# Second layer of a streaming encoder: where the output projection of two token tiles stands

## The chip, the cores and the metric

The kernel runs on one core of one Trainium2 chip. The metric is the device time of one launch in microseconds (us). A core has five engines with a queue each: TensorE (PE, matmuls; PEld is its weight load), VectorE (DVE), ScalarE (ACT), GpSimd (POOL) and SyncE (SP, which only issues DMAs). Each executes its instructions in the order in which they stand, and waits for the others by semaphores. In TensorE's accumulators (PSUM, here banks of 128x512 floats) the products arrive; SBUF holds operands; DRAM the inputs, outputs and spilled tiles.

## What is computed

Two layers over 1024 prompt frames and 8 streams of 16 new frames: attention (the first layer with a sliding window, the second over its own and eight earlier chunks of 64 frames), the output projection with a residual, and a squared-ReLU MLP. For the second layer, cut to what matters here:

```python
qp = project_q_b(hp, g_attn[layer], w_q_b[j], g_q_b[j])
ap = band_attention_prompt(qp, kb_p, vb_p, LEFT_CHUNKS_B, rel_fn, None)
hp = hp + ap @ w_o_b[j]
hp = hp + mlp(hp, g_mlp[layer], w_up[layer], w_down[layer])
```

`mlp` begins with an RMS norm over the 1024 features: the mean of squares of a row, its inverse root, and a multiplication with the gain. Results are float32; each operand is split into a rounded high part and the rest, and a product is three matmuls (high x high, high x low, low x high).

## The kernel before

The frames are nine tiles of 128 rows: tiles 0 to 7 of the prompt, tile 8 (`ST`) of the samples. Attention works in 32 groups, one per tile and pair of steps over the four K/V heads: the first 16 groups take heads 0 and 1 of all tiles, the last 16 heads 2 and 3. For a group, scores are computed in two halves (`score_b`, L388: matmuls L400, minimum and bias on DVE L424 to L428, exponentials on ACT L437 and L440, the sum's reciprocal L447, the division on POOL L450), the probabilities are turned by PE (L293), split (ACT L109, DVE L115) and multiplied with V (L300, L301); ACT copies the result (L315) and SP stores it (L320).

The output projection follows the same halves. The half `A` (heads 0 and 1, the first 512 rows of the weight) and the half `B` (the last 512 rows) of a tile each load the stored attention output in two parts (L306, L308), add them (L310), split the sum into `oh` and `ol`, and run 24 matmuls, 12 for each 512 columns (`wo_proj`, L144 to L149). In attention `WO` (L1474) does this: it loads the residual tile (L1497), adds each half row of the product to it on DVE (L1508) and stores it (L1510, on POOL's queue for the half B); its addition L310 and its cast of `oh` (L111) run on POOL. The table `plan` of `CFG` tells after which group a tile's half is taken; what is listed under 32 comes after the last group (`run(work_of(32))`, L1699). Whatever stands in `plan` under B goes into `wo_done`; tiles whose home in `xt` is `keep` stay in SBUF (tiles 0 and 4).

Behind attention comes the passage ahead of the MLP, `wo_phase` (L612). It goes through the nine tiles in the order of `WO_ORDER`, for this layer 0, 4, 1, 5, 6, 2, 7, 3, 8. `O` loads the residual tile (L629) and, if its half B is not done, the attention output. `M` does the missing half B: 24 matmuls into `ps_wo`, two additions on DVE (L653), a store on ACT's queue (L655), and then for every tile the norm (L602): squares on ACT (L605), a small DVE step (L607), the inverse root on POOL (L609) and, in place, the scaling on DVE (L610). When both tiles of a pair (i, i + 4) are ready, `S` forms four sums and differences on POOL (L669 to L672) and `T` turns seven half tiles by PE (L662) and splits them (ACT L109, DVE L115) into `sx`. The up products (L715 to L717) read `sx` and the split weights of the first block, loaded by L743 into `ru` and split into `wq` and `w`.

Nobody writes the order of the instructions by hand: a scheduler puts each engine's work in order from priorities and its own model of durations. The lines that matter for the order are these:

```python
run(work_of(32))
self.wo_done = {t for g in plan for c, t in plan[g] if c == "B"}
```

```python
for n in range(2) if t not in self.wo_done else ():
    nn = slice(n * 512, n * 512 + 512)
    ps = self.psum("m", [P, 512], "ps_wo")
    self.wo_proj(ps, *osp[t], wo, nn)
    nc.vector.tensor_tensor(x[:, nn], ps, x[:, nn], ALU.add)
if t not in self.wo_done:
    nc.scalar.dma_start(self.xd[t], x)
```

Of the kernel before, what the change touches and what calls it, by code (L numbers as in the profile page):

```python
# [1709 lines left out]
def make_plan(tail):  # L1710
    plan = {}
    for s in range(2 * NT):
        if s + 2 < NT:
            plan[2 * s] = [("Q", s + 2)]
        elif s + 2 < 2 * NT:
            plan[2 * s] = [("R", s + 2 - NT)]
        if s + 3 < NT:
            plan[2 * s + 1] = [("K", s + 3)]
    plan[13] = [("R", ST)]
    plan.update(tail)  # L1720
    return plan
# [27 lines left out]
CFG = [  # L1749
    dict(banks=dict(g=(5, 1), s=(2, 1), m=(1, 1)), q_bufs=4, order={}, plan=make_plan({15: [('A', 0)], 17: [('A', 1)], 19: [('A', 2)], 21: [('A', 3)], 23: [('A', 4)], 25: [('A', 5)], 30: [('A', 6)], 31: [('A', 7)], 32: [('A', 8), ('B', 0), ('B', 4), ('B', 3)]}),  # L1750
        la=3, prio=0, xt={('A', 8): 'x', ('B', 3): 'x', ('B', 0): 'keep', ('B', 4): 'keep'}, late=0, eng='cgu', k2=3, q2=9, lead=3, sf=0, up=(99, 2, 0, 3), ld=((10, 10, 11, 11), (11, 12, 13, 14), (27, 28, 29, 30)), n='g', q='g', qrb=1, np=3, bias_bufs=3, p_bufs=3, psp=(), wr='mmmm', wt=(0, 0, 2, 0, 2, 2, 0, 1, 2), rx=1, kd=1, o2=0, sb=0),
    dict(banks=dict(g=(4, 1), s=(3, 1), m=(1, 1)), q_bufs=4, order={}, plan=make_plan({15: [('A', 0)], 17: [('A', 1)], 19: [('A', 2)], 21: [('A', 3)], 23: [('A', 4)], 25: [('A', 5)], 27: [('A', 8)], 28: [('A', 7)], 29: [('A', 6)], 31: [('B', 0), ('B', 4), ('B', 1)], 32: [('B', 5), ('B', 2), ('B', 3)]}),
        la=2, prio=1000, xt={('B', 0): 'keep', ('B', 4): 'keep', ('B', 1): 'hh', ('B', 5): 'hl', ('B', 2): 'hh', ('B', 3): 'hl'}, late=0, eng='Ogu', k2=3, q2=6, lead=9, sf=0, up=(4, 2, 0, 99), ld=((11, 11, 11, 11), (11, 11, 11, 11), (26, 27, 28, 29)), n='g', q='g', qrb=2, np=2, bias_bufs=2, p_bufs=10, psp=(), wr='mmmm', wt=(0, 0, 0, 1, 1, 1, 1, 1, 2), rx=0, kd=1, o2=1, sb=3),
]

TC_KW = dict(schedule_with_timeline_sim=True)
# [42 lines left out]
```

## Time and profile before

| | us |
|---|---|
| three runs, median | 2405.27 |
| lowest and highest | 2404.04, 2407.24 |
| span of the profiled execution, first to last instruction | 2399.3 |

The profile gives the profiled execution by its span alone; its own launch time is not listed, so the 6.0 us between the span and the median stand for what lies around the span. The profile is of one execution. It lists for each engine when an instruction ran, how long it took, and how long the engine stood idle before it, with the instruction or the transfer that ended that idle time. PE's busy share is 97%, DVE's 68%, ACT's 51%, POOL's 22%. The mean granted TensorE clock is 0.992 of full speed.

### The profile page before, as it was taken

To read this page: it belongs to the slowest core of one execution; us is meant where nothing else is said; L and a number is where in the kernel's file an instruction comes from. 1 tells how busy PE (TensorE), PEld (TensorE's weight loads), DVE (VectorE), ACT (ScalarE), POOL (GpSimd) and SP (SyncE) were. 2 spreads that over 40 slices of the span, in tenths; PEclk is the share of its full clock that TensorE was granted. 3 is DMA by queue.
4 is the path that set the end of the run, shared out by engine and by line. 5 is a ranking of instruction groups with operands and counts; after the bars stand their busy time and mean duration, and the time that the engine had idled before them with its cause. 6 is when DMAs were issued, how large, how long until landed. Compare 5 with 4: busy or idle time off the path is not lost.

```text
span 2399.3 us, 33421 instructions
## 1 busy us (share of the span) xinstructions
PE 2320.4 (97%) x11621; PEld 1935.5 (81%) x11621; DVE 1626.3 (68%) x3002; ACT 1217.9 (51%) x2423; POOL 535.6 (22%) x828
## 2 busy tenths in 40 slices
PE   7998999899999999999999999998999999999999
PEld 6786877788888888888777788887888888888887
DVE  6687786755655777776567877877655555776674
ACT  4676675555555433232267666665655555333321
POOL 3343332312112100000333434344211211000000
PEclk9998999999999999999999999999999999999999
DMA  7345546244433874342743555555434435744332
GB/s 244 122 127 168 171 156 200 95 155 158 145 128 141 323 245 146 117 141 99 237 149 111 188 161 173 173 169 174 138 127 145 154 137 200 278 140 158 112 116 114
DMA packets 218457, 385.88 MB, mean 161 GB/s; under 512 B 50408, under 2 KB 125104, under 8 KB 211120
## 3 DMA queue, kind: packets, MB, share of 16 engines
q1 hardware_dynamic: 195136, 307.16, 39.0%
q0 software_dynamic: 21776, 71.84, 7.7%
q10 hardware_dynamic: 1376, 4.74, 0.5%
q8 instruction: 92, 1.51, 0.3%
q14 instruction: 77, 0.63, 0.1%
HBM read 246.47 MB, written 136.14 MB: 159 GB/s over the span
## 4 chain that ended last, share of the span: by engine, by line
PE 82%; DMA 7%; DVE 5%; ACT 2%; issue 2%; POOL 1%; SPq 1%; ACTq 0%; DVEq 0%; POOLq 0%
PE ps_x L715 9%; PE ps_x L717 9%; PE ps_x L716 9%; PE ps_y L717 7%; PE ps_y L716 7%; PE ps_y L715 7%; PE ps_mm L186 3%; PE ps_mm L188 3%; PE ps_mm L187 3%; PE ps_tr L293 2%; PE ps_mm L147 2%; PE ps_mm L149 2%; PE ps_mm L148 2%; PE ps_s L717 1%; PE ps_s L716 1%
## 5 line engine op out<-in xcount | busy, mean ns | idle before, releaser
L109 ACT CAST w<-r 128x2048 fp32r<-128x2048 f32 x56 | 107.1, 1913 | 322.9 <-PE ps_y L717 212.1
L715 PE MATMUL ps_x<-w,s 128*128 128x512 f32 x512 | 199.5, 390 | 2.7 <-DVE hc L854 2.1
L717 PE MATMUL ps_x<-w,s 128*128 128x512 f32 x512 | 199.4, 389 | 0.0
L716 PE MATMUL ps_x<-w,s 128*128 128x512 f32 x512 | 199.2, 389 | 0.0
L186 PE MATMUL ps_mm<-w,hh 128*128 128x512 f32 x432 | 175.0, 407 | 13.8 <-ACT kw L253 5.1
L188 PE MATMUL ps_mm<-w,hl 128*128 128x512 f32 x432 | 174.3, 403 | 1.7 <-DMA hl<-hTd 1.4
L187 PE MATMUL ps_mm<-w,hh 128*128 128x512 f32 x432 | 172.5, 400 | 0.7 <-DVE w L159 0.7
L109 ACT CAST s<-s 128x2048 fp32r<-128x2048 f32 x56 | 107.1, 1913 | 117.9 <-DMA s<-hd 108.6
L115 DVE TENSOR_TENSOR w<-r,w 128x2048 fp32r<-128x2048 f32 x56 | 128.2, 2290 | 51.9 <-ACT w L109 51.9
L715 PE MATMUL ps_x<-sx,w 128*128 128x512 f32 (+1 forms) x408 | 157.8, 387 | 4.6 <-ACT hc L834 2.7
L1021 DVE TENSOR_TENSOR x<-ps_y,x 128x512 f32<-128x512 f32 x136 | 92.3, 687 | 101.1 <-PE ps_y L717 101.0
L717 PE MATMUL ps_x<-sx,w 128*128 128x512 f32 (+1 forms) x408 | 154.1, 378 | 0.0
L716 PE MATMUL ps_x<-sx,w 128*128 128x512 f32 (+1 forms) x408 | 154.1, 378 | 0.0
L109 ACT CAST w<-ru 128x512 fp32r<-128x512 f32 (+1 forms) x160 | 110.0, 708 | 85.3 <-PE ps_y L716 32.0
L717 PE MATMUL ps_y<-w,s 128*128 128x512 f32 x384 | 149.5, 389 | 0.0
L716 PE MATMUL ps_y<-w,s 128*128 128x512 f32 x384 | 149.4, 389 | 0.0
L715 PE MATMUL ps_y<-w,s 128*128 128x512 f32 x384 | 149.4, 389 | 0.0
L115 DVE TENSOR_TENSOR s<-s 128x2048 fp32r<-128x2048 f32 x56 | 128.1, 2287 | 26.5 <-ACT s L109 26.5
L115 DVE TENSOR_TENSOR ptl<-ps_tr,pth 128x512 fp32r<-128x512 f32 x180 | 122.6, 685 | 24.8 <-ACT pth L109 19.0
L115 DVE TENSOR_TENSOR w<-ru,w 128x512 fp32r<-128x512 f32 (+1 forms) x160 | 126.6, 793 | 10.9 <-ACT w L109 10.8
L109 ACT CAST pth<-ps_tr 128x512 fp32r<-128x512 f32 x180 | 104.8, 594 | 47.9 <-PE ps_tr L293 39.3
L115 DVE TENSOR_TENSOR wq<-ru,wq 128x1024 fp32r<-128x1024 f32 x32 | 39.7, 1240 | 131.9 <-ACT wq L109 131.9
(280 smaller groups left out, 6573.3 us busy)
## 6 DMA issues: line engine op xcount, KB each, us to landing
s<-hd SPq DMA_DIRECT2D x56, 1024.0 KB, 4.7
ru<-in_w_up SPq DMA_DIRECT2D x64, 512.0 KB, 3.9
r<-in_w_down SPq DMA_DIRECT2D x32, 1024.0 KB, 5.7
hd<-hc POOLq DMA_DIRECT2D x128, 256.0 KB, 2.7
hd<-hs POOLq DMA_DIRECT2D x96, 256.0 KB, 2.5
x<-xd SPq DMA_DIRECT2D x41, 512.0 KB, 4.6
o<-oTd SPq DMA_DIRECT2D x52, 256.0 KB, 4.1
hTd<-hh SPq DMA_DIRECT2D x36, 256.0 KB, 4.5
```

The lines of the kernel that those rows point to most:

```text
L109: a = nc.scalar.copy(hi, src)
L115: return a, e.tensor_tensor(lo, src, hi.bitcast(F32), ALU.subtract)
L147: nc.tensor.matmul(ps, oh[:, k, :], w[:, 0, k, nn], start=(k == 0), stop=False)
L148: nc.tensor.matmul(ps, oh[:, k, :], w[:, 1, k, nn], start=False, stop=False)
L149: nc.tensor.matmul(ps, ol[:, k, :], w[:, 0, k, nn], start=False, stop=(k == 3))
L186: nc.tensor.matmul(ps, a, w[:, 0, k, :], start=(k == 0), stop=False)
L187: nc.tensor.matmul(ps, a, w[:, 1, k, :], start=False, stop=False)
L188: nc.tensor.matmul(ps, b, w[:, 0, k, :], start=False, stop=(k == KC - 1))
L715: a = mm(ps, ah, bh, start=first, stop=False, skip_group_check=True)
L716: mm(ps, ah, bl, start=False, stop=False, skip_group_check=True)
L717: return a, mm(ps, al, bh, start=False, stop=last, skip_group_check=True)
L1021: tt(xs[t][:, N[n]], ps, xs[t][:, N[n]], ALU.add)
```

## The change

In the second layer's entry of `CFG`, the tiles 2 and 3 of the half B are taken out of `plan` under 32, and their homes out of `xt`. Nothing else is edited. So `WO` is not called for them at the end of attention, they are no longer in `wo_done`, and `wo_phase` does their half B, in its order (6, 2, 7, 3, 8), with its own instructions: the addition of the two parts and the cast of `oh` then run on DVE and ACT, and the store is issued by ACT.

```diff
-    dict(banks=dict(g=(4, 1), s=(3, 1), m=(1, 1)), q_bufs=4, order={}, plan=make_plan({15: [('A', 0)], 17: [('A', 1)], 19: [('A', 2)], 21: [('A', 3)], 23: [('A', 4)], 25: [('A', 5)], 27: [('A', 8)], 28: [('A', 7)], 29: [('A', 6)], 31: [('B', 0), ('B', 4), ('B', 1)], 32: [('B', 5), ('B', 2), ('B', 3)]}),
-        la=2, prio=1000, xt={('B', 0): 'keep', ('B', 4): 'keep', ('B', 1): 'hh', ('B', 5): 'hl', ('B', 2): 'hh', ('B', 3): 'hl'},
...
+    dict(banks=dict(g=(4, 1), s=(3, 1), m=(1, 1)), q_bufs=4, order={}, plan=make_plan({15: [('A', 0)], 17: [('A', 1)], 19: [('A', 2)], 21: [('A', 3)], 23: [('A', 4)], 25: [('A', 5)], 27: [('A', 8)], 28: [('A', 7)], 29: [('A', 6)], 31: [('B', 0), ('B', 4), ('B', 1)], 32: [('B', 5)]}),
+        la=2, prio=1000, xt={('B', 0): 'keep', ('B', 4): 'keep', ('B', 1): 'hh', ('B', 5): 'hl'},
...
```

What the scheduler makes of it shows in the engines' orders. The first place is PE at the end of attention, ahead of the second half of the last group's scores (`ps_sf`, `ps_sn`); `ps_mm` is the projection. Before:

```order
L301 MATMUL ps_pv<-ptl,VS 128x512
L293 MATMUL ps_tr<-identr,p 128x128 x5
L147 MATMUL ps_mm<-w,oh 128x512
L148 MATMUL ps_mm<-w,oh 128x512
L149 MATMUL ps_mm<-w,ol 128x512
...
L400 MATMUL ps_sf<-KT,qT 128x384 x4
L400 MATMUL ps_sn<-KT,qT 128x256 x4
```

And now, at the same place:

```order
L293 MATMUL ps_tr<-identr,p 128x128 x5
L301 MATMUL ps_pv<-ptl,VS 128x512
L400 MATMUL ps_sf<-KT,qT 128x384 x4
L300 MATMUL ps_pv<-pth,VS 128x512
L400 MATMUL ps_sn<-KT,qT 128x256 x4
```

The twelve projection matmuls (three rows shown, repeated four times) no longer stand between the transposes and the scores; the same holds for three more groups of twelve behind them.

The second place is DVE in the passage, where a tile's second addition and its norm stand. Before, `x_17389` is tile 7, `x_17322` tile 2 and `x_17303` tile 6:

```order
L653 TENSOR_TENSOR x_17389<-ps_wo_17512,x_17389 128x512
L653 TENSOR_TENSOR x_17389<-ps_wo_17526,x_17389 128x512
L610 SCALAR_TENSOR_TENSOR x_17322<-x_17322,mrs_17444,gb_11010 128x1024
L610 SCALAR_TENSOR_TENSOR x_17303<-x_17303,mrs_17434,gb_11010 128x1024
L115 TENSOR_TENSOR sx_17188<-ps_n_17296,sx_17187 128x4x128
L115 TENSOR_TENSOR sx_17223<-ps_n_17340,sx_17222 128x4x128
L115 TENSOR_TENSOR sx_17218<-ps_n_17347,sx_17217 128x4x128
L607 TENSOR_SCALAR mms_17544<-mssq_17542 128x1
L610 SCALAR_TENSOR_TENSOR x_17389<-x_17389,mrs_17546,gb_11010 128x1024
```

And now, `x_17223` being tile 6, `x_17242` tile 2 and `x_17318` tile 7:

```order
L310 TENSOR_TENSOR o_17368<-o_17368,o2_17370 128x512
L653 TENSOR_TENSOR x_17242<-ps_wo_17377,x_17242 128x512
L607 TENSOR_SCALAR mms_17361<-mssq_17359 128x1
L610 SCALAR_TENSOR_TENSOR x_17223<-x_17223,mrs_17363,gb_11010 128x1024
L115 TENSOR_TENSOR sx_17108<-ps_n_17216,sx_17107 128x4x128
L115 TENSOR_TENSOR sx_17143<-ps_n_17269,sx_17142 128x4x128
L115 TENSOR_TENSOR sx_17138<-ps_n_17276,sx_17137 128x4x128
L653 TENSOR_TENSOR x_17242<-ps_wo_17391,x_17242 128x512
L115 TENSOR_TENSOR ol_17374<-o_17368,oh_17373 128x512
L653 TENSOR_TENSOR x_17318<-ps_wo_17479,x_17318 128x512
L607 TENSOR_SCALAR mms_17409<-mssq_17407 128x1
L610 SCALAR_TENSOR_TENSOR x_17242<-x_17242,mrs_17411,gb_11010 128x1024
```

Between a tile's second addition and its norm fewer instructions stand than before: two and the small step L607 for tile 2, and the same for tile 7 further on; one addition and L607 for tile 3.

The third place is SP's queue where attention ends (`oTd_1_7_109` is the attention output of tile 7, `xd_113` the residual of tile 2). Before:

```order
L320 DMA oTd_1_7_109<-pvt 64x2x128 x8
L306 DMA o<-oTd_1_7_109 128x512
L588 DMA oTd_1_8_110<-so 128x2x32
L308 DMA o_17393<-oTd_1_7_109 128x512
L743 DMA ru<-in_w_up 128x4x256 x2
L629 DMA x<-xd_113 128x1024
```

And now:

```order
L320 DMA oTd_1_7_109<-pvt 64x2x128 x4
L306 DMA o<-oTd_1_3_105 128x512
L320 DMA oTd_1_7_109<-pvt 64x2x128 x4
L743 DMA ru<-in_w_up 128x4x256 x2
L306 DMA o<-oTd_1_7_109 128x512
L308 DMA o_17322<-oTd_1_7_109 128x512
```

The loads of the up weights moved ahead of those of tile 7's attention output, and a load for tile 3 came in.

## Rows read from the trace of the kernel before

**Rows 1.** The page's first part: busy us, share of the span, instructions.

```profile
PE 2320.4 (97%) x11621; PEld 1935.5 (81%) x11621; DVE 1626.3 (68%) x3002; ACT 1217.9 (51%) x2423; POOL 535.6 (22%) x828
```

**Rows 2.** Busy time by stretch (us from the span's start), tail and passage.

```profile
core 0: us, PE busy (x) PEld busy (x) DVE busy (x) ACT busy (x) POOL busy (x), PEclk, DMA share, GB/s
1600.00:1642.00 42.00, 38.57 (x210) 31.93 (x210) 30.20 (x71) 25.71 (x70) 16.20 (x22) 1.00 0.51 167
1642.00:1664.90 22.90, 22.71 (x122) 18.50 (x121) 16.88 (x25) 11.46 (x22) 13.07 (x10) 1.00 0.70 223
1664.90:1690.80 25.90, 17.46 (x104) 14.07 (x104) 23.03 (x35) 17.05 (x31) 12.50 (x11) 0.87 0.22 78
```

**Rows 3.** PE's timeline in the tail: start, us, instruction, idle before and its end.

```profile
1617.12 0.50 PE L147 MATMUL ps_mm<-w,oh 128*128 128x512 f32 x1 [1.53 <-DVE mms L607]
...
1619.97 0.87 PE L400 MATMUL ps_sf<-KT,qT 128*128 128x384 f32 x4
```

**Rows 4.** Timelines of DVE, ACT and POOL in the tail.

```profile
1627.62 0.69 DVE L310 TENSOR_TENSOR o<-o,o 128x512 f32<-128x512 f32 x1 [2.19 <-DMA o<-oTd]
1629.01 0.17 DVE L447 RECIPROCAL li<-l 128x2 f32<-128x2 f32 x1
1641.08 2.46 DVE L610 SCALAR_TENSOR_TENSOR xo<-xo,mrs,gb 128x1024 f32<-128x1024 f32 x2
1626.48 0.47 ACT L440 ACTIVATE p<-ps_sn,mnb 128x256 f32<-128x256 f32 x1
1637.52 0.59 ACT L109 CAST pth<-ps_tr 128x512 fp32r<-128x512 f32 x1 [2.38 <-PE ps_tr L293]
1629.32 0.61 POOL L1510 DMA_DIRECT2D xd<-xo  x1 [6.50 <-DVE li L447]
1629.98 1.58 POOL L450 TENSOR_SCALAR p<-p,li 128x640 f32<-128x640 f32 x2
```

**Rows 5.** DVE's timeline in the passage: splits of turned tiles.

```profile
1645.54 1.89 DVE L115 TENSOR_TENSOR sx<-ps_n,sx 128x512 fp32r<-128x512 f32 x3 [1.99 <-ACT sx L109]
1691.69 0.69 DVE L115 TENSOR_TENSOR sx<-ps_n,sx 128x512 fp32r<-128x512 f32 x1
```

**Rows 6.** Busy time by stretch: the first layer's whole passage, then the second layer's.

```profile
396.20:457.80 61.60, 55.63 (x313) 46.11 (x311) 49.77 (x74) 31.82 (x56) 26.89 (x24) 1.00 0.43 144
1641.10:1692.30 51.20, 42.20 (x238) 34.28 (x238) 42.31 (x63) 30.37 (x56) 25.57 (x21) 0.93 0.46 151
```

**Rows 7.** SP's and ACT's timelines: tile 7's stores, the up weights' loads and cast.

```profile
1634.67 10.27 SPq L320 DMA_DIRECT2D oTd<-pvt  x8
1647.03 0.92 SPq L743 DMA_DIRECT2D ru<-in_w_up  x2
1651.81 1.06 ACT L109 CAST wq<-ru 128x1024 fp32r<-128x1024 f32 x1
```

**Rows 8.** DVE's additions and norms: tiles 7 and 8, then the first layer.

```profile
1659.80 1.29 DVE L653 TENSOR_TENSOR x<-ps_wo,x 128x512 f32<-128x512 f32 x2 [1.10 <-DMA x<-xd]
1666.38 1.28 DVE L610 SCALAR_TENSOR_TENSOR x<-x,mrs,gb 128x1024 f32<-128x1024 f32 x1 [1.04 <-DMA xd<-x]
1671.79 1.27 DVE L653 TENSOR_TENSOR x<-ps_wo,x 128x512 f32<-128x512 f32 x2
1676.15 1.28 DVE L610 SCALAR_TENSOR_TENSOR x<-x,mrs,gb 128x1024 f32<-128x1024 f32 x1 [0.95 <-DMA xd<-x]
435.20 0.68 DVE L653 TENSOR_TENSOR x<-ps_wo,x 128x512 f32<-128x512 f32 x1
439.59 1.28 DVE L610 SCALAR_TENSOR_TENSOR x<-x,mrs,gb 128x1024 f32<-128x1024 f32 x1 [0.95 <-POOL mrs L609]
```

**Rows 9.** Line 655 in the passage, three stores: us from issue to landing.

```profile
DMA to landing us min/median/max: 2.6/5.2/6.5
```

**Rows 10.** Busy time by stretch, columns as in rows 2: granted clock.

```profile
1660.00:1670.00 10.00, 6.71 (x36) 5.04 (x34) 8.89 (x12) 5.31 (x10) 3.27 (x5) 1.00 0.51 158
1670.00:1680.00 10.00, 8.16 (x43) 7.59 (x44) 8.71 (x14) 4.75 (x9) 6.65 (x6) 0.66 0.13 52
```

More of the change, by code (lines that the diff above doesn't have):

```diff
@@ L1751 @@
         la=3, prio=0, xt={('A', 8): 'x', ('B', 3): 'x', ('B', 0): 'keep', ('B', 4): 'keep'}, late=0, eng='cgu', k2=3, q2=9, lead=3, sf=0, up=(99, 2, 0, 3), ld=((10, 10, 11, 11), (11, 12, 13, 14), (27, 28, 29, 30)), n='g', q='g', qrb=1, np=3, bias_bufs=3, p_bufs=3, psp=(), wr='mmmm', wt=(0, 0, 2, 0, 2, 2, 0, 1, 2), rx=1, kd=1, o2=0, sb=0),
-    dict(banks=dict(g=(4, 1), s=(3, 1), m=(1, 1)), q_bufs=4, order={}, plan=make_plan({15: [('A', 0)], 17: [('A', 1)], 19: [('A', 2)], 21: [('A', 3)], 23: [('A', 4)], 25: [('A', 5)], 27: [('A', 8)], 28: [('A', 7)], 29: [('A', 6)], 31: [('B', 0), ('B', 4), ('B', 1)], 32: [('B', 5), ('B', 2), ('B', 3)]}),
-        la=2, prio=1000, xt={('B', 0): 'keep', ('B', 4): 'keep', ('B', 1): 'hh', ('B', 5): 'hl', ('B', 2): 'hh', ('B', 3): 'hl'}, late=0, eng='Ogu', k2=3, q2=6, lead=9, sf=0, up=(4, 2, 0, 99), ld=((11, 11, 11, 11), (11, 11, 11, 11), (26, 27, 28, 29)), n='g', q='g', qrb=2, np=2, bias_bufs=2, p_bufs=10, psp=(), wr='mmmm', wt=(0, 0, 0, 1, 1, 1, 1, 1, 2), rx=0, kd=1, o2=1, sb=3),
+    dict(banks=dict(g=(4, 1), s=(3, 1), m=(1, 1)), q_bufs=4, order={}, plan=make_plan({15: [('A', 0)], 17: [('A', 1)], 19: [('A', 2)], 21: [('A', 3)], 23: [('A', 4)], 25: [('A', 5)], 27: [('A', 8)], 28: [('A', 7)], 29: [('A', 6)], 31: [('B', 0), ('B', 4), ('B', 1)], 32: [('B', 5)]}),
+        la=2, prio=1000, xt={('B', 0): 'keep', ('B', 4): 'keep', ('B', 1): 'hh', ('B', 5): 'hl'}, late=0, eng='Ogu', k2=3, q2=6, lead=9, sf=0, up=(4, 2, 0, 99), ld=((11, 11, 11, 11), (11, 11, 11, 11), (26, 27, 28, 29)), n='g', q='g', qrb=2, np=2, bias_bufs=2, p_bufs=10, psp=(), wr='mmmm', wt=(0, 0, 0, 1, 1, 1, 1, 1, 2), rx=0, kd=1, o2=1, sb=3),
 ]
```

## Prediction, written before the changed kernel ran

> **What bounds the kernel now.** I read the busy shares first [rows 1]: PE is busy 97% of the span of 2399.3 us, so PE's idle time in the stretch that the change touches is all that can be won or lost, some ten microseconds. Then I cut the second layer's turn from attention to the MLP into three stretches [rows 2]. In the tail of attention (1600 to 1642 us) PE is busy 38.57 of 42.00 us. In the first part of the passage (1642 to 1664.9), where the output projection of tiles 6, 7 and 8 runs, it is busy 22.71 of 22.90. In the second part (1664.9 to 1690.8) it is busy only 17.46 of 25.90, and DVE 23.03: there DVE sets the pace, with the splits of the turned tiles, the norms and the split of the first weights. So the change takes matmuls from a stretch with 3.4 us of idle PE and puts them, with their DVE work, ahead of a stretch that DVE bounds.
>
> **Removed from the tail.** Tiles 2 and 3 have two half rows of 12 matmuls each, 48 in all. Twelve take 2.85 us, from 1617.12 to 1619.97 [rows 3]: 11.4 us of PE together. They did not all lie on the path; three places give something back.
> (a) The first group stands ahead of the last scores. The order shows those scores now right behind the transposes: 2.8 us.
> (b) The last exponentials end at 1626.95, but the division of the probabilities ends only at 1631.56 [rows 4]: DVE sits idle for 2.19 us until 1627.62 for a tile of the projection, adds it, and POOL puts a store of 0.61 us ahead. In the new order none of this is in front of the reciprocal; it needs 0.17 us, the division 1.58 us, and about 0.5 us of hand-overs: 4.6 becomes 2.3, a gain of 2.3 us.
> (c) The last group stands among the transposes of the last head group; ACT waits 2.38 us for them [rows 4]. That goes: 2.4 us.
> Sum 7.5 us. Bounds: at most the whole 11.4; at least 3.8, if (c) is taken up by the two casts that ACT now has there and a norm of 1.28 us that DVE now runs between two score reductions comes off (a) (2.3 + 1.5).
>
> **Removed DMAs.** Two loads of x and two stores on POOL's queue go from the tail; the stores come back on ACT's queue in the passage, and the loads are the ones the passage had anyway. I cost this at nothing beyond (b). The first o load of tile 2 now stands early in SP's queue, held until the first half's last projection matmul; that matmul ends ahead of the store that stands behind it, so nothing waits longer.
>
> **Added to the passage.** I measure it from the two norms of the kept tiles (DVE, 1641.08) to the last split of turned tiles, which ends at 1692.3 [rows 4, 5]: 51.2 us, in which DVE is busy 42.31 and idle 8.9 [rows 6].
> Work: four additions of the projection, one addition of two o halves and one split of it (those of tile 2 fall ahead of 1641.08 in the new order). Three DVE instructions in a row take 1.89 us [rows 5], so 0.63 each: 3.8 us. PE's 11.4 us fit: it is busy 42.2 of 51.2 us now [rows 6].
> Waits at the start: DVE idles 1.99 us for the first turned tile, as before [rows 5]. Its next instruction was an addition; now it is the split of the first up weights. Their load goes out right behind the last stores of tile 7, which end 3.9 us after the start; the cast began 4.8 us after the issue (1647.03 to 1651.81) and takes 1.06 [rows 7], so the split starts near 10.0 us after the start, while DVE is free at 6.3: 3.7 us idle, 5.7 together.
> Waits in front of norms: the norm works in place, so it waits for the store of the same tile and for its own statistics. From the end of the second addition to the norm's start it took 5.3 us for tile 7 (1661.09 to 1666.38) and 3.1 us for tile 8 (1673.06 to 1676.15), both ended by the store, and 3.7 us once in the first layer [rows 8]. The spread is the landing of the stores, 2.6 to 6.5 us [rows 9], longer while loads fly. Before, six instructions or more stood between and little idling was left. Now, by the order, between the second addition and the norm DVE has 2.0 us of work for tile 6, 1.4 for tiles 2 and 7, 0.8 for tile 3 and 3.2 for tile 8. I take 5.3 for tiles 6 and 2, whose stores go out while other tiles load, and 3.1 for 7, 3 and 8, which come when the loads are through: 3.3 + 3.9 + 1.7 + 2.3 + 0 = 11.2 us idle.
> Idle sum 16.9 us against 8.9, so 8.0 more; with the work 11.8 us. Bounds: with 5.3 for all five, 17.7 idle in front of norms and 18.3 us in all. Low: the first layer's passage is the nearest row without such an order; it holds 84 more of these matmuls (20.0 us) and is 61.6 us long instead of 51.2 [rows 6], 0.52 us for each us of PE, which for 11.4 us gives 5.9.
> The row shows landings of 2.6 to 6.5 us. The Trainium skill (DMA: Bandwidth & Descriptors, Anatomy of one DMA) fits a fixed 2.0 us and bytes over 436 GB/s for the software path, an estimate of 3.2 us for 512 KB whatever else flies. By that rule, with 0.4 us to the issue, all five norms would wait 3.6 us, 9.2 us idle, and the time would be 2.0 us less, 2407.6; the longest landing speaks against it.
>
> **Sum.** -7.5 + 11.8 = +4.3 us on the profiled span of 2399.3. The median of the three runs, 2405.27, stands 6.0 us above that span, for what lies around it, and the change does not touch that: 2409.6 us. Only above 0.2% (4.8 us) could a measurement of this kernel tell it from no change, so this lies just inside.
>
> **The rivals.**
> Faster, PE-bound throughout: the whole 11.4 us leaves the tail, and the passage grows as in the first layer, 5.9: -5.5, 2399.8 us. For it: PE is full in the tail and in the first part. Against: the waits of DVE and ACT in the tail [rows 4] are not PE's, and the order puts norms right behind additions.
> Same, with the scheduler's idle filled: tail 7.5, passage 5.9: -1.6, 2403.7 us. For it: DVE has 8.9 us of idle, and the first layer does twice as many tiles with only 11.8.
> Slower, by the stores: loads fly through the whole passage, so every norm waits 5.3 us: -7.5 + 18.3 = +10.8, 2416.1 us. It decides where the store of tiles 7, 3 and 8 lands later than 3.9 us after its issue, halfway. For it: the landing's median of 5.2 us. Against: tile 8's was short.
> Slower, by the clock: between 1660 and 1670 PE was busy 6.71 us of 10, and in the next 10 us the granted clock was 0.66, a mean over the two levels 2.4 and 1.2 GHz [rows 10]. There only turns and 256-wide products stood, off the path. If it falls in the new passage while the projection runs, a third of 10 us is lost to PE, 3.4 us, on top of the forecast: +7.7, 2413.0 us. The Trainium skill (TensorE: Matmul & The Clock Gate, Part 1) says that an idle TensorE is halved and only sustained work gives the clock back; the trace agrees, 0.66 behind idle time.
> That the change does not do what it says is ruled out by the order: 24 matmuls of each of the two tiles now stand behind the end of attention.
>
> **How the numbers follow.** Forecast 0.48, with its own range of 2405 to 2414 (each wait between its short and its long value); faster 0.13; same 0.18; stores 0.11; clock 0.10. The forecast straddles the bound of 4.8 us, a little over half inside: 0.26 same, 0.22 slower. Slower 0.22 + 0.11 + 0.10 = 0.43; same 0.26 + 0.18 = 0.44; faster 0.13. The range of 2402 to 2416 leaves out most of the faster rival and half of the stores', under 0.2.
>
> **What would show it.** The start of the passage (the two kept norms) should come near 1633.6 in the new profile. From there to the last split of turned tiles should be near 63 us, with DVE idle near 17 and rows in which the norm waits for a store of x of tiles 6, 2, 7 and 3. The second half of the last scores should start near 1617. It is wrong if the passage is under 58 us, if its idle time stands in front of other instructions than these norms and the weight split, or if the tail ends where it did.

## The result, and the profile after

| | before | changed |
|---|---|---|
| 22 runs each, median, us | 2403.8 | 2410.8 |
| lowest and highest, us | 2394.6, 2410.6 | 2404.8, 2417.2 |
| ratio, with its 95% interval | | 1.0026 (1.0016 to 1.0036) |
| span of the profiled execution, us | 2399.3 | 2405.7 |

By the ratio the changed kernel is 6.3 us slower (3.9 to 8.7; the medians are 7.0 apart). The forecast was +4.3. The interval is clear of zero, but it does not settle whether the change costs more than 4.8 us, which the prediction took as the least that can be told from no change. The profiled execution of the changed kernel took 2407.47 us by its launch time and 2405.7 by its span, so 1.8 us lie around a span. Of the 6.0 us that the prediction put "around the span", 4.2 are only the distance of that execution from the median.

The page's first part for the changed kernel, then its windows over the end of attention and the passage (columns as in [rows 2]):

```profile
PE 2321.5 (97%) x11621; PEld 1935.2 (80%) x11621; DVE 1630.3 (68%) x3004; ACT 1218.6 (51%) x2425; POOL 531.5 (22%) x822
```

```profile
1623.60:1633.60 10.00, 6.05 (x27) 3.58 (x26) 7.46 (x14) 6.05 (x13) 0.57 (x1) 1.00 0.54 171
1633.60:1638.60 5.00, 4.16 (x20) 3.47 (x21) 3.86 (x5) 2.91 (x8) 2.44 (x2) 0.66 0.40 108
1633.60:1698.30 64.70, 53.98 (x285) 44.14 (x285) 48.84 (x69) 29.47 (x57) 24.88 (x21) 0.92 0.40 137
```

The last line answers to the second of [rows 6]: the passage, from the kept norms to the last split of turned tiles, is 64.7 us long instead of 51.2, with 48.8 us of DVE work instead of 42.3 and 15.9 us of DVE idle time instead of 8.9. The first two lines are new: PE is busy only 6.05 of the last 10 us of attention, and in the next 5 us, the first of the passage, the granted clock is 0.66. Before, both the tail and the first part of the passage stood at 1.00 [rows 2].

What DVE waited for in the passage, in total, times and longest (the view of waits):

```profile
DVE x L610 <- DMA xd<-x: 6.8, 4, 3.7
DVE sx L115 <- ACT sx L109: 4.4, 6, 2.0
DVE wq L115 <- ACT wq L109: 2.4, 1, 2.4
DVE mms L607 <- ACT junk L605: 2.1, 4, 1.0
```

DVE's timeline there, the kept norms and then the norms of tiles 6, 2, 7, 3 and 8, which answer to [rows 8]:

```profile
1633.62 2.46 DVE L610 SCALAR_TENSOR_TENSOR xo<-xo,mrs,gb 128x1024 f32<-128x1024 f32 x2
...
1654.36 1.80 DVE L610 SCALAR_TENSOR_TENSOR x<-x,mrs,gb 128x1024 f32<-128x1024 f32 x1 [1.17 <-DMA xd<-x]
...
1663.97 1.28 DVE L610 SCALAR_TENSOR_TENSOR x<-x,mrs,gb 128x1024 f32<-128x1024 f32 x1 [3.67 <-DMA xd<-x]
...
1670.39 1.98 DVE L610 SCALAR_TENSOR_TENSOR x<-x,mrs,gb 128x1024 f32<-128x1024 f32 x1 [0.99 <-DMA xd<-x]
...
1677.49 1.95 DVE L610 SCALAR_TENSOR_TENSOR x<-x,mrs,gb 128x1024 f32<-128x1024 f32 x1 [0.99 <-DMA xd<-x]
...
1688.06 1.28 DVE L610 SCALAR_TENSOR_TENSOR x<-x,mrs,gb 128x1024 f32<-128x1024 f32 x1
```

The chain of work that ended last, from tile 6's second addition on (start, us, what):

```profile
1650.74 0.61 DVE x L653
...
1651.37 2.90 DMA xd<-x
...
1656.09 1.87 DVE sx L115 x3
1657.96 0.61 DVE x L653
...
1658.60 5.29 DMA xd<-x
...
1665.18 1.88 DVE sx L115 x3
1667.06 0.61 DVE x L653
...
1667.69 2.61 DMA xd<-x
...
1672.29 1.88 DVE sx L115 x3
1674.16 0.61 DVE x L653
...
1674.80 2.60 DMA xd<-x
...
1677.49 1.95 DVE x L610
```

It is one figure four times over: second addition, store, its landing, norm in place, three splits, next second addition. The landings alone are 13.4 us of the chain. The longest is tile 2's store (5.29), the only one under which loads of x flew (tiles 3 and 8, issued at 1655.11 and 1657.62).

### The profile page after: what moved, and what is told of

It is laid out like the page before. It is cut to its first block, busy times and chain, and to the rows that moved or that the text cites. A ratio compares the mean times of both kernels' runs of the same rounds, so it can differ in the third digit from the quotient of the medians.

```text
span 2405.7 us, 33408 instructions
## 1 busy us (share of the span) xinstructions
PE 2321.5 (97%) x11621; PEld 1935.2 (80%) x11621; DVE 1630.3 (68%) x3004; ACT 1218.6 (51%) x2425; POOL 531.5 (22%) x822
## 4 chain that ended last, share of the span: by engine, by line
PE 80%; DMA 8%; DVE 6%; ACT 3%; issue 2%; POOL 1%; SPq 1%; ACTq 0%; DVEq 0%; POOLq 0%
PE ps_x L715 9%; PE ps_x L717 9%; PE ps_x L716 9%; PE ps_y L716 7%; PE ps_y L717 7%; PE ps_y L715 7%; PE ps_mm L186 3%; PE ps_mm L188 3%; PE ps_mm L187 3%; PE ps_tr L293 2%; PE ps_mm L147 2%; PE ps_mm L149 1%; PE ps_mm L148 1%; PE ps_s L717 1%; PE ps_s L716 1%
## 5 line engine op out<-in xcount | busy, mean ns | idle before, releaser
L115 DVE TENSOR_TENSOR w<-r,w 128x2048 fp32r<-128x2048 f32 x56 | 128.3, 2291 | 52.2 <-ACT w L109 52.2
L115 DVE TENSOR_TENSOR w<-ru,w 128x512 fp32r<-128x512 f32 (+1 forms) x160 | 126.6, 794 | 11.3 <-ACT w L109 11.2
```

Of the source, the lines that this page charges most:

```text
L115: return a, e.tensor_tensor(lo, src, hi.bitcast(F32), ALU.subtract)
```

## The experiments

Executions differ by 15 us in the time at which the same instructions ahead of the change run, so the spans of two profiles say little. The table counts from one reciprocal of attention's sums (L447, the eighth from the last; 1572.15 us in the first profile of before, 1568.85 in that of the change) to the kept norms, then the passage, and then to L845, the MLP's first addition into `ps_y`. "Timed" is the ratio times the median of before in the same comparison, with its interval.

| kernel | kept norms at | passage | L845 at | timed against before, us |
|---|---|---|---|---|
| before, two profiles | 68.9, 68.1 | 51.3, 49.8 | 124.1, 121.8 | |
| the change, two profiles | 64.8, 64.6 | 64.7, 63.2 | 133.8, 132.0 | +6.3 (3.9 to 8.7) |
| tail alone | 65.5 | 55.8 | 127.0 | -1.4 (-4.6 to +1.9) |
| no store | 64.8 | 59.6 | 130.1 | +1.7 (-1.7 to +5.1) |
| before, no store | 68.9 | 51.9 | 124.7 | +1.0 (-2.2 to +4.3) |
| norm later | 64.5 | 56.9 | 127.0 | +2.9 (-0.2 to +6.0) |
| additions late | 63.8 | 63.9 | 132.1 | +9.8 (6.5 to 13.0) |
| tile 3 alone | 68.0 | 56.0 | 129.8 | +4.1 (1.4 to 7.0) |
| tile 6 too | 69.3 | 52.7 | 125.8 | +3.8 (0.5 to 7.4) |
| before, norm later | 69.5 | 52.4 | 125.8 | +3.1 (0.0 to 6.2) |
| tile 6 and norm later | 68.0 | 53.4 | 125.3 | +4.6 (1.9 to 7.2) |

From L845 to the end of the span it is 703.0 to 703.6 us in every profile: nothing behind is changed. Three of the kernels leave something out: tail alone the half B of tiles 2 and 3, the two without stores the stored residual of the second layer's passage.

**The two kernels once more.**

> The changed kernel itself, profiled once more, to see how far one execution speaks for the others. Counted from the third but last group's reciprocal of the sum (L447, the 57th of the execution), the kept norms came at 64.8 us, the last split of turned tiles ended at 129.4 and the MLP's first addition into ps_y (L845) stood at 133.8. Stores theory: kept norms within 1 us of that, the end within 3 us, as the landing of four stores varies; the half clock at the start of the passage comes again. Rival, the 3.7 us wait for tile 2's store was an accident: the end comes 3 us or more earlier.

> The kernel before, profiled once more: from the same reciprocal the kept norms came at 68.9 us, the last split ended at 120.2 and L845 stood at 124.1. Expected within 1.5 us of these. If L845 comes at 127 or later, the first profile was a lucky one and the change costs 6 us there, not 9.7.

The kept norms came within 0.8 us and the passages within 1.5 us of their first profiles; only L845 of the kernel before was off by more than named, 2.3 us earlier, which makes the difference no smaller. The clock over its passage was 0.97 instead of 0.93. In the changed kernel the clock fell again at the start of the passage, to 0.52 in its first 5 us. The wait for tile 2's store is no accident; the second profile has it at 4.53 us:

```profile
1671.14 1.28 DVE L610 SCALAR_TENSOR_TENSOR x<-x,mrs,gb 128x1024 f32<-128x1024 f32 x1 [4.53 <-DMA xd<-x]
```

By these profiles the change takes 3.8 us from the tail, adds 13.4 to the passage and 0.4 behind it: +9.9, more than the timed +6.3. That two profiles of each kernel stand above the interval of the timed runs stays open. So it is for two variants: at L845, tail alone stands 4.0 us and no store 7.1 us behind the mean of before, against -1.4 and +1.7 timed. The profiles are used below for where the time goes, the timed runs for what a version costs.

**The tail alone.**

```diff
+            if layer:
+                self.wo_done |= {2, 3}
```

> The changed kernel, with the half B of tiles 2 and 3 left out altogether (their residual lacks heads 2 and 3); they pass through the passage like tiles 1 and 5. It weighs the tail of attention alone. Stores theory (the tail gives 7.5 us, the passage takes 13.5 because each norm of a moved tile stands behind the store of its own tile): the two kept norms start near 1633.6, the passage is 49 to 52 us long, as before the change (51.2) or less by the wait of tile 2, and the time is 7.5 to 9 us under the kernel before. Rival, the start of the passage (the first split of up weights now waits 2.4 us for its load, which would stay here): the passage stays 54 us or longer and the time is 3 to 5 us under.

Neither number was met. The kept norms came 3.1 us earlier than before (65.5 against the mean of 68.5), not 7.5, and the passage was 55.8 us long though it had nothing of tiles 2 and 3 to compute. Its windows, two in the tail and then three from the passage on:

```profile
1622.97:1627.97 5.00, 3.56 (x17) 2.85 (x17) 4.17 (x14) 3.81 (x11) 0.61 (x1) 0.82 0.31 118
1627.97:1632.97 5.00, 4.96 (x26) 3.68 (x24) 2.71 (x7) 3.61 (x13) 2.21 (x4) 0.84 0.62 170
...
1643.00:1648.00 5.00, 4.20 (x18) 3.54 (x19) 3.82 (x5) 2.69 (x7) 2.48 (x3) 0.53 0.35 85
1643.00:1698.80 55.80, 43.77 (x229) 36.50 (x230) 45.76 (x63) 30.12 (x56) 26.82 (x21) 0.84 0.41 139
1693.00:1703.00 10.00, 7.40 (x40) 6.53 (x39) 7.28 (x12) 5.15 (x11) 0.00 (x0) 0.66 0.65 211
```

The granted clock fell in the tail itself, to 0.82 and 0.84; it is 0.53 in the first 5 us of the passage, 0.84 over the passage instead of 0.93 [rows 6], and 0.66 where the MLP's products begin. But what grew in the passage is above all DVE's work: 63 instructions, as many as before, keep it busy 45.8 us instead of 42.3 [rows 6], and it idles 10.0 us instead of 8.9. Three norms of 1.28 us took 2.10, 2.27 and 2.04 us beside sums that POOL forms; the next runs show this more plainly. So this run does not weigh the tail by itself, and what the clock alone cost in it is not shown. The rival had the right length, but for another reason: the split of the first weights did not wait in this run. 11.4 us of PE work left out of the program gave 1.4 us, with zero inside the interval.

**Without the stores**, in the changed kernel and in the kernel before.

```diff
-                if t not in self.wo_done:
+                if t not in self.wo_done and not layer:
                     nc.scalar.dma_start(self.xd[t], x)
```

> The changed kernel without the store of the residual in the second layer's passage (tiles 6, 2, 7, 3, 8), so that nothing holds the norm back but its own statistics; the second layer's last addition then reads a residual without half B of these tiles. Stores theory: the four waits of norms (6.8 us of DVE's idle time) shrink to the 0.9 us or so of the statistics' way over ACT and POOL, PE gets its turns earlier, and the time falls by 4 to 7 us against the changed kernel, so near the kernel before (0 to +2 us). Rival, the added work (DVE's six instructions and PE's 11.4 us set the length whatever the stores do): it falls by less than 1.5 us, +5 us against the kernel before.

> The kernel before, without the same stores (tiles 6, 7, 8). Stores theory: it has two waits of 1.0 us behind stores, of which the statistics would leave a part, so it gains 0 to 2 us against itself. Rival, the stores cost by their traffic (they slow the loads of x that fly beside them): it gains 3 us or more, since tile 2's load, on the chain for 9.7 us, lands earlier.

The changed kernel lost 4.6 us of its 6.3, as the stores theory said, though the two intervals overlap and L845 came only 2.8 us earlier. The kernel before gained nothing that can be seen, so no cost of the stores' traffic by itself shows. But the passage was still 59.6 us long, with DVE's idle time down to 8.6 us and its busy time up to 51.0:

```profile
1643.70:1703.30 59.60, 52.33 (x280) 42.81 (x281) 51.00 (x69) 29.55 (x57) 24.74 (x21) 0.93 0.32 105
```

The norms, no longer held back, now ran into the sums that POOL forms. One of four such pairs, DVE's row and then POOL's:

```profile
1663.65 2.31 DVE L610 SCALAR_TENSOR_TENSOR x<-x,mrs,gb 128x1024 f32<-128x1024 f32 x1
```

```profile
1663.58 1.29 POOL L672 TENSOR_TENSOR s<-x,s 128x512 f32<-128x512 f32 x1
```

The norm takes 1.28 us where POOL is idle, and here 2.31: the rest of POOL's sum (until 1664.87) and 1.09 us behind it.

**The norm later.** `M` and the norm are separated, so that a tile's norm is written behind the next tile's projection, and ordered on DVE behind its second addition:

```diff
-                M(t)
+                M(m)
+                N(t, m)
...
+            def N(t, m):
+                    y = self.norm(small, work.tile([P, D], mybir.dt.bfloat16, tag="junk", name="junk"), xs[t])
+                        self.behind(added[m], y)
```

> The changed kernel; in the second layer the norm of a stored tile is ordered behind the second addition of the next tile (an order of DVE's instructions only, no buffer and no instruction added), so that 2 to 5 us of other work stand between a store and its norm. Stores theory: the waits of 1.2, 3.7, 1.0 and 1.0 us go, the passage is 58 to 61 us instead of 64.7, and the time is 4 to 7 us under the changed kernel, within 2 us of the kernel before. Rival, the added work: same length, 64 us, +6 us. Second rival, turns that come later: the norm and with it the turns of a pair come 2 us later each, PE runs out of projection at the end, and the time is over the changed kernel's.

One wait of 1.21 us for a store is left of four, and the passage is 56.9 us, shorter than expected. The second rival fell: no buffer and no work was taken away, only the place of the norm. DVE idles 8.8 us, where it was 8.9 before the change [rows 6]; what is left of the growth is DVE's work, 48.1 us instead of 42.3 (first row). 3.4 of the 6.3 us came back in the timed runs, less than the 4 to 7 expected, with intervals that overlap; in the profiles L845 came 5.9 us earlier, after 1.3 us were given back behind the passage (5.6 us to L845 instead of 4.3). PE has done its projection by 1684 and is then busy only in part, until the MLP's products start at the lower clock:

```profile
1644.00:1700.90 56.90, 50.09 (x277) 41.62 (x278) 48.14 (x70) 30.71 (x57) 24.10 (x21) 0.93 0.50 169
1694.00:1704.00 10.00, 5.87 (x30) 4.91 (x31) 7.12 (x12) 5.27 (x10) 0.00 (x0) 0.66 0.62 210
```

**The additions of the halves late.**

```diff
+                if layer and y is not None:
+                    self.behind(self.kept_norm, y)
```

> The changed kernel, with the additions of the o halves (L310) of the passage ordered on DVE behind the two kept norms (order alone). In the profile of the changed kernel the first of them waits 2.8 us for its load, ahead of the last head group's splits, on DVE, and ACT's cast behind it waits too. If that took the gain (c) from the tail: the kept norms come 2 to 3 us earlier (62 to 63 us from the reciprocal instead of 64.8), and the time falls by as much, unless the passage's projection then starts later. Rival, the tail ends with the chain of the last head group's own transposes, casts and products: no change, kept norms at 64 to 65.

The kept norms came 0.8 us earlier, not 2 to 3, and the time did not fall: +9.8 with an interval that overlaps the change's. But the tail does not end with the last head group's own work either, as the rival had it. Another load takes the place of the one that was ordered away: ACT's squares for a norm wait for their tile of x, with the casts of the last head group behind them:

```profile
1629.97 1.06 ACT L605 ACTIVATE junk<-x 128x1024 bf16<-128x1024 f32 x1 [2.01 <-DMA x<-xd]
```

The start of the passage is of use here, too: the last 10 us of the tail and the next 5 us in this run, then the first 5 us of the passage in the run with the later norm.

```profile
1625.88:1635.88 10.00, 6.24 (x31) 4.03 (x31) 5.04 (x11) 5.01 (x11) 1.17 (x2) 1.00 0.50 155
1635.88:1640.88 5.00, 3.88 (x24) 2.74 (x25) 4.31 (x6) 3.35 (x9) 2.46 (x2) 1.00 0.34 72
...
1644.02:1649.02 5.00, 4.18 (x22) 3.68 (x22) 3.84 (x5) 2.98 (x8) 2.46 (x2) 0.66 0.45 117
```

Here the clock stayed at 1.00 and the passage was still 63.9 us, with 5.4 us of waits for stores, though four more instructions of DVE stand in it, the ones that were moved there (73 against 69). With the later norm the clock fell as in the changed kernel, and the passage was 56.9 us. So the half clock at the start is not what makes the passage long.

**Tile 3 alone.** (From the entry of `plan`; tile 2's home in `xt` goes with it.)

```diff
-32: [('B', 5)]}
+32: [('B', 5), ('B', 2)]}
```

> Only tile 3 moved into the passage; tile 2's half B is done at the end of attention as before the change. If the cost goes by the tile: half of the change, +2 to +4 us against the kernel before. Rival, the tail only gives its time back when the last group of the projection is gone from it (that of the second listed tile), and the passage takes one store wait per tile: the tail gives all 4 us for one tile, the passage takes 6 to 7, so +2 to +3 as well but with kept norms at 65. Third, the passage has room for one tile (8.9 us of DVE's idle time): within 1 us of the kernel before.

The first theory holds as far as the noise lets one say: +4.1 us (1.4 to 7.0) for one tile. The second fell, since the kept norms came at 68.0 us and not at 65, and so did the third, since the interval leaves out anything under 1.4 us. The tail gives 0.5 us, the passage takes 5.4. Here no norm waits for a store; DVE's waits in the passage were for casts of turned tiles and for a load:

```profile
DVE sx L115 <- ACT sx L109: 6.3, 6, 2.0
DVE o L310 <- DMA o<-oTd: 1.8, 1, 1.8
DVE x L610 <- POOL mrs L609: 1.1, 2, 0.7
```

So a tile's work has its price without any wait for a store; those waits come with the second tile.

**The other direction, and a version that might beat both.** Tile 6's half B, too, at the end of attention; the later norm on the kernel before; both together.

```diff
-32: [('B', 5), ('B', 2), ('B', 3)]}
+32: [('B', 5), ('B', 2), ('B', 3), ('B', 6)]}
```

> The reverse of the change: to the kernel before, the half B of a third tile, 6, is added at the end of attention, and taken from the passage. Counted from the same reciprocal, no tile moved into the passage gave L845 at 121.8 and 124.1 us, one tile (3) 129.8, two (2, 3) 132.0 and 133.8. If the cost goes on by the tile (some 5 us each): the passage is 45 to 48 us, the kept norms come 1 to 5.7 us later (24 matmuls of 0.24 us are 5.7), and the time is 0 to 4 us under the kernel before. Rival, the data of tile 6 come too late for the tail: its attention output is stored in the last but one group, so its addition, on POOL here, stands in front of the last division or its projection behind the end of attention, where it brings its matmuls in front of the first turns: 2 us or more over the kernel before.

> The kernel before, with the norm of a stored tile ordered behind the next tile's second addition, as in the run of the changed kernel. Stores theory: it has two waits of 1.0 us behind stores, so 0 to 2 us under the kernel before. Rival, later turns: PE has nothing to do between its last projection and the first turn of the pair of tile 2 and 6 already (0.66 of 5 us busy, then the half clock); a norm that comes later makes this longer: 1 to 3 us over.

> Tile 6 at the end of attention and the later norms together. If both theories hold, the sum of the two runs, and the candidate for the fastest version: 2 to 5 us under the kernel before. If tile 6 comes too late for the tail, over it by 1 us or more.

None is faster: +3.8, +3.1 (with zero at the edge of its interval) and +4.6 us, as the rivals said. Tile 6's data come too late for the tail; the second half row of its projection stands behind the first turns, inside the passage (PE's timeline):

```profile
1643.03 1.04 PE L662 MATMUL ps_n<-identr,xo 128*128 128x128 f32 x8
...
1645.20 0.47 PE L147 MATMUL ps_mm<-w,oh 128*128 128x512 f32 x1
```

In the kernel before the later norm has little to win, since its two waits are 1.0 us each [rows 8]. What it costs there was not taken apart. Of the versions that compute the whole layer, none is faster than the kernel before.

## Why the prediction was nearly right

The sign was right, and so was the mechanism in the passage; the tail was sized too large. The sum was 2.0 us under the timed value. By the profiles both terms erred the same way, the tail by 3.7 us and the passage by 1.6, and the whole is +9.9; so it is in part luck that the timed value lies this near.

**The tail, -7.5 forecast, -3.8 measured.** The mean over two profiles of each is at the lower bound that the prediction named, 3.8.
(a) 2.8 became 2.3, measured to the end of the last exponentials: 52.2 us behind the reciprocal in both profiles, 54.8 and 54.3 before. The second half of the last scores starts at 44.4 us instead of 47.8, but its third matmul waits for ACT's exponentials, so that its last one ends only 1.1 us earlier; the rest is won from there to the exponentials' end (4.1 us instead of 5.6).

```profile
1615.20 0.62 PE L400 MATMUL ps_sf<-KT,qT 128*128 128x384 f32 x2 [1.44 <-ACT p L437]
```

(b) was nearly right. From the end of the last exponentials (1621.00) to the end of the last division it is 2.5 us instead of 4.6 (4.3 in the second profile of before); 2.3 was forecast.

```profile
1621.96 1.58 POOL L450 TENSOR_SCALAR p<-p,li 128x640 f32<-128x640 f32 x2 [1.85 <-ACT so L587]
```

(c) is the step that failed. From the end of the division to the kept norms it is 10.1 us now and was 9.5 before, where 7.1 was forecast. ACT's wait of 2.38 us among the transposes [rows 4] was on the path. The chain of work of the kernel before runs through the last group of the projection into them:

```profile
1636.59 0.23 PE ps_mm L149
1636.82 0.23 PE ps_pv L300
1637.04 0.44 PE ps_tr L293 x4
```

But what was taken out is filled by loads, which the prediction cost at nothing. DVE's wait in front of the reciprocal (2.19 us, in (b)) is for tile 6's attention output, and it does not go with tiles 2 and 3: both kernels store this output in the last group but one and load it at once. DVE's addition of its halves started 55.5 us behind the reciprocal before [rows 4] and starts at 56.2 now, behind the division instead of in front of it, and ahead of the last head group's splits:

```profile
1625.06 0.69 DVE L310 TENSOR_TENSOR o<-o,o 128x512 f32<-128x512 f32 x1 [2.77 <-DMA o<-oTd]
```

With the additions of the halves ordered away 9.4 us are left, and in tail alone 8.9: there ACT waits for a tile of x (2.01 and 0.96 us) ahead of the same group's casts.

**The passage, +11.8 forecast, +13.4 measured.** Its idle part was 7.0 us against 8.0 forecast. The idle time in front of the norms of tiles 6, 2, 7, 3 and 8 came out at 1.2, 4.1, 1.4, 2.0 and 0.3 us (stores 6.8, squares 2.1): 8.9 against 11.2, with tile 2 the longest, as forecast. From the second addition to the norm it took 3.0, 5.4, 2.7 and 2.7 us for the first four, where the prediction had 5.3, 5.3, 3.1 and 3.1. The landings themselves were 2.9, 5.3, 2.6 and 2.6 us. The fit that the Trainium skill gives for the software path (DMA: Bandwidth & Descriptors, Anatomy of one DMA) makes an estimate of 3.2 us for any 512 KB. These stores went out on ACT's queue, and their landings lie on both sides of it. At the start DVE idled 4.4 us, 2.4 of them for the weight split, where 5.7 and 3.7 were forecast. Not forecast are some 2 us more of waits for casts of turned tiles at the end.
The work grew by 6.4 us where the prediction had 3.8. The six instructions cost 4.1 at 0.68 us each; the rest comes mostly from instructions that got longer beside POOL's sums: L775 from 0.68 to 1.65 us, L776 from 0.68 to 1.19, one L310 from 0.69 to 1.78, three norms from 1.28 to 1.80, 1.98 and 1.95. That is 4.5 us in all, where the kernel before has 1.8 of the kind. Its trace had such a row in plain sight, but the prediction did not ask why:

```profile
1668.39 2.28 DVE L610 SCALAR_TENSOR_TENSOR x<-x,mrs,gb 128x1024 f32<-128x1024 f32 x1
```

**Stores or work.** The later norm leaves 6.3 us of the passage's growth (56.9 against the mean of 50.6) with DVE's idle time back at 8.8 us, and the low bound of the prediction, the first layer's 0.52 us for each us of PE, was 5.9. So about half of the 13.4 us is the price of the work, as in the first layer, and about half goes with the norm's place behind its own store.

**The rivals.** Faster, PE-bound throughout, is refuted by the passage, and "same" by the store waits. The stores' rival fell with the landings for tiles 7, 3 and 8, 2.6 us each where it needed more than 3.9; that its +10.8 is near the profiles' +9.9 is chance. The clock rival was right in kind and wrong in place. The clock fell not while the projection ran but at the start of the passage, behind a tail in which PE was busy 6.05 of 10 us; from the kept norms to the first `ps_wo` matmul it took 5.0 us instead of 3.6. In additions late PE was busy 6.24 of 10 us there, the clock stayed at 1.00, and it took 3.8 us. So idle time alone does not decide it, and what does stays open.

**What would show it.** The kept norms at 1633.62 (1633.6 was named) are right by luck, since this execution was 3.3 us ahead at the reciprocal. The second half of the last scores (near 1617 named) starts at 1613.25, which with these 3.3 us is 1616.6. The passage (63 named, 64.7 and 63.2 found) and DVE's idle time (17 named, 15.9) are right by their steps.

## What to carry to other kernels

Matmuls that fill another stage's holes are worth more than their place on the path shows: they can hold the clock, and they keep their own additions, stores and norms out of a stage that another engine bounds. What is taken off the chain of work is a gain only down to the next wait that ends there; look for loads that stand ahead of the same work in the other engines' queues before counting it. Where an instruction works in place on a tile that is being stored, count the landing of the store into its start, or put another tile's work between.

## What the runs showed of the hardware that was not expected

DVE's norm and POOL's elementwise sums exclude each other, in both directions. In the kernel without stores a norm from 1677.23 to 1679.54 met a sum that ran until 1678.46, and the next sum of POOL took 2.29 us instead of 1.29:

```profile
1677.23 2.31 DVE L610 SCALAR_TENSOR_TENSOR x<-x,mrs,gb 128x1024 f32<-128x1024 f32 x1
```

```profile
1678.40 2.29 POOL L672 TENSOR_TENSOR s<-x,s 128x512 f32<-128x512 f32 x1
```

The Trainium skill (SBUF — State Buffer, SBUF: two separate sides) says that DVE with two SBUF inputs and a GpSimd instruction that reads SBUF hold a common port in turn, each for a whole instruction; these rows agree. DVE's splits of turned tiles, which take one operand from PSUM, are not held: in the changed kernel three of them took 1.88 us from 1672.29 on, beside a sum that ended at 1673.53, as elsewhere. The second surprise is that leaving 48 matmuls out bought next to nothing, 1.4 us (-1.9 to 4.6): the granted clock fell to 0.84 over the passage, and DVE's work there grew by 3.4 us.
